# Strided attention on one core: query block 0 loaded ahead of the keys, and the first stores and reused loads in another order

## The chip, the cores and the metric

The kernel runs on one core of one Trainium2 chip. The metric is the device time of one execution in microseconds (us); the number that counts is the median of several executions. A profiled execution is recorded beside them, with its own time and with the span from its first to its last instruction.

## What is computed

Q, K and V have shape 8 x 12 x 1024 x 64 in float32, and the stride is 64. Every query attends to the same 16 positions of its head, which are rows 0, 64, 128 and so on of K and V:

```python
batch, heads, seq, dim = Q.shape              # 8, 12, 1024, 64
attend_positions = np.arange(0, seq, stride)  # 16 positions
k = K[:, :, attend_positions, :]
v = V[:, :, attend_positions, :]
scores = np.einsum('bhqd,bhkd->bhqk', q, k) / np.sqrt(dim)
weights = softmax(scores)                     # over the 16 positions
result = np.einsum('bhqk,bhkd->bhqd', weights, v)
```

All of Q is read (25.2 MB), of K and V one row of 256 bytes in 64 (0.39 MB each), and the result is as large as Q (25.2 MB).

## The kernel before

**Tiles.** The 96 heads are worked on in 24 groups of 4 heads. One group's queries are 1 MiB, 8 KB in each of 128 partitions. The tile `big` has 16 such buffers (NB = 16); group g uses buffer g modulo 16. A group's outputs are written into the buffer that its queries came in, and are stored from there. So groups 0 to 15 each have a buffer from the start, and groups 16 to 23 reuse the buffers of groups 0 to 7: their loads, the *reused loads*, can be issued only when the outputs of the old group have been stored. Keys and values are loaded into the last buffer (`k_raw`, `v_raw` are views of it), and are rearranged with the help of the one before it; queries 14 and 15 are loaded there later.

**The work of one group.** ACT and POOL each convert half of the queries to bfloat16 (`cast_a` on line 343, `cast_p` on line 348), DVE transposes them (`turn_over`, line 352), PE makes the scores (line 505), DVE transposes them and takes the maximum (lines 372 and 377), POOL subtracts it, ACT takes the exponential (line 388), DVE adds up and inverts, POOL normalises, DVE transposes the weights, PE makes the outputs (line 519) in two halves, and ACT copies each half into `big` (`evict`, line 420). A loop over n runs these steps skewed: step n holds the score work of group n, the casts of later groups (`cast_a(n + 3)`, `cast_p(n + 2)`) and the outputs of groups n - 2 and n - 3.

**The keys' way.** ACT casts the first half of the key rows and POOL the second (lines 289 and 290), DVE transposes them (line 292), DVE and ACT lay them out in `k_all` (line 299), and POOL copies a group's part into `k_cur` (line 356). Value rows are cast by POOL (line 314) and spread over the partitions by PE (line 306).

**What sets the order.** The kernel is one list of operations, written by hand in the order of the code. `op` records each with what it reads and writes; `plan` derives the semaphore waits. Each engine runs its own operations in the order of the list. All transfers are issued by SP, one after the other, on one queue; a transfer that must wait for a semaphore holds SP, and with it every later transfer. The `lane` of a transfer is the semaphore that it raises when it has landed: `q0` to `q15` for the loads, `out0` to `out7` for the stores (and for K and V, which borrow three of them).

**The transfers.** A load of queries (`load`) and a store (`store`, `send`) are issued through `_copy` (line 34), which writes the DMA instruction itself. A load reads 32 runs of 32 KB; a store takes two groups, 2 MiB. K and V go through the ordinary call `nc.sync.dma_start` (line 254) with 128 rows of 256-byte pieces. `first_loads` issues K in two halves, then queries 0, then V, then queries 1 to 13; queries 14 and 15 follow within the loop. After that the list `order` says in which order stores ("S") and reused loads ("L") are issued; `issue` is called at the end of each step and takes from the head of the list whatever is due. The store of group g waits for an ACT operation behind the eviction of the group (`at_ACT`); the reused load of group g waits for the store that frees its buffer. The very last store, of groups 22 and 23, is issued after the loop (line 560).

Of the kernel before, what the change touches and what calls it, by code (L numbers as in the profile page):

```python
# [18 lines left out]
def _ap_with(ap: bass.AP, new_ap, extra_offset: int = 0) -> bass.AP:  # L19
    return dataclasses.replace(  # L20
        ap, ap=[list(p) for p in new_ap], offset=ap.offset + extra_offset
    )
# [20 lines left out]
class Program:  # L43
# [13 lines left out]
    def op(self, engine, fn, reads=(), writes=(), after=(), lane=None, gate=None, gates=(), looped=False, last=False):  # L57
        i = len(self.ops)
        deps, own = set(after), set()
        for k in reads:  # L60
            deps.add(self.writer.get(k))
            own.add(self.writer.get(k))
        for k in writes:
            deps.update(self.readers.get(k, ()))
            deps.add(self.writer.get(k))
            own.add(self.writer.get(k))
        deps.discard(None)
        for k in reads:
            self.readers.setdefault(k, []).append(i)
        for k in writes:  # L70
            self.writer[k], self.readers[k] = i, []
        self.ops.append(dict(
            engine=engine, fn=fn, lane=lane or engine, deps=deps, own=own,
            gate=gate, gates=gates, last=last, looped=looped or engine == "PE",
        ))
        return i
# [90 lines left out]
def kernel(  # L167
# [8 lines left out]
    nc = tc.nc  # L176

    B, H, S, D = Q.shape
# [3 lines left out]
    P = 128  # L182
# [3 lines left out]
    NC = NG // 2  # L186
    SD = S * D
    NB = 16
# [10 lines left out]
    big = sb.tile([P, NB, 32 * D], FP32, name="big")  # L199
# [19 lines left out]
    k_raw = spare[:, 0 : NC * D].rearrange("p (n d) -> p n d", d=D)  # L219
    v_raw = spare[:, NC * D : 2 * NC * D].rearrange("p (n d) -> p n d", d=D)  # L220
    later_bf = later.bitcast(BF16)
    k_bf, k_r, v_bf, v_rep, v_rep2 = [
        later_bf[:, i * NC * D : (i + 1) * NC * D].rearrange("p (n d) -> p n d", d=D) for i in range(5)
    ]
# [5 lines left out]
    op = prog.op  # L230

    def load(g):
        n, b = 32, g % NB
        over = {NB - 1: ["k_raw0", "k_raw1", "v_raw"], NB - 2: ["k_bf0", "k_bf1", "k_r", "v_bf", "v_rep0", "v_rep1"]}
        op("SP", lambda: _copy(
            nc, big[:, b], _ap_with(Q, [[HG * SD // n, n], [1, HG * SD // n]], g * HG * SD),
        ), writes=[f"b{b}a", f"b{b}b"] + (over.get(g) or []), lane=f"q{b}")

    def store(g, n):
        b = g % NB  # L240
        op("SP", lambda: send(g, n), lane=f"out{b // 2}",
           reads=[f"b{i % NB}{h}" for i in range(g, g + n) for h in "ab"])

    def send(g, n):
        o = big[:, g % NB : g % NB + n]
        return _copy(
            nc,
            _ap_with(out, [[16 * D, P], [2 * SD, 2 * n], [1, 16 * D]], g * HG * SD),
            _ap_with(o, [o.ap[0], [1, 1], [1, 32 * n * D]]),
        )  # L250

    def first_loads():
        def rows(name, tile_, src, i0, n, lane):
            op("SP", lambda: nc.sync.dma_start(tile_[:, i0 : i0 + n], _ap_with(  # L254
                src, [[stride * D, P], [2 * HG * SD, n], [1, D]], 2 * HG * SD * i0,
            )), writes=[name], lane=lane)

        for m in range(2):
            rows(f"k_raw{m}", k_raw, K, NC // 2 * m, NC // 2, f"out{5 + m}")
        load(0)  # L260
        rows("v_raw", v_raw, V, 0, NC, "out7")
        for g in range(1, NB - 2):
            load(g)

    def constants():
# [20 lines left out]
        ), reads=["identity"], writes=["s_sel"])  # L286

    def key_rows():
        op("ACT", lambda: nc.scalar.copy(k_bf[:, 0:6], k_raw[:, 0:6]), reads=["k_raw0"], writes=["k_bf0"])
        op("POOL", lambda: nc.gpsimd.tensor_copy(out=k_bf[:, 6:], in_=k_raw[:, 6:]),  # L290
           reads=["k_raw1"], writes=["k_bf1"])
        op("DVE", lambda: nc.vector.transpose(
            k_r.rearrange("p n d -> p (n d)").bitcast(I32), k_bf.rearrange("p n d -> p (n d)").bitcast(I32),
        ), reads=["k_bf0", "k_bf1"], writes=["k_r"])
# [122 lines left out]
    def evict(g, h):  # L417
# [3 lines left out]
           gate=None if g == NG - 1 else "ev")  # L421

    first_loads()
    constants()
    key_rows()
    for s in range(4):
        keys(0, s, "DVE" if s < 2 else "ACT")
# [3 lines left out]
    for s in range(4):  # L431
# [8 lines left out]
    value_copy(1)  # L440
    cast_a(2)
    value_blocks(0, range(2))
    order = [("S", 0), ("S", 2), ("S", 4), ("L", 16), ("L", 17), ("S", 6), ("L", 18), ("L", 19), ("S", 8),
             ("L", 20), ("L", 21), ("S", 10), ("L", 22), ("L", 23)] + [("S", g) for g in range(12, 22, 2)]

    def issue(done, flush=False):
        while order:
            kind, g = order[0]
            need = g + (kind == "S") if kind != "L" else g - NB + 1
            if not flush and need > done:  # L450
                return
            order.pop(0)
            if kind == "L":
                load(g)
            else:
                store(g, 2)

    def on(f, g, *a):
        if 0 <= g < NG:
# [135 lines left out]
```

## Time and profile before

| | |
|---|---|
| median of 3 executions | 128.47 us (128.4 to 129.09) |
| profiled execution, its own time | 128.98 us |
| profiled execution, span | 127.2 us |
| bytes moved by DMA | 51.18 MB, mean 402 GB/s |
| busy share of the span: PE, DVE, ACT, POOL | 52%, 77%, 71%, 68% |
| mean granted TensorE clock | 0.767 |
| loads of queries, stores, loads of K, loads of V | 24, 12, 2, 1 |

In the rows of the profile, L343 is line 343 of the kernel before, `big<-in_Q_dram` a load of queries, `out_dram<-big` a store. A row of the timeline gives the start, the duration, the engine, the line, the operation, what it writes and reads, how many of them, and in brackets how long the engine had been idle before it and what ended that. A table of windows gives the busy time of each engine in stretches of the span, the granted clock (PEclk), the DMA share (mean busy share of the 16 DMA engines, by the packets that start in the stretch, so it can exceed 1) and the rate.

### The profile page before, as it was taken

What the parts mean: (1) busy time and instruction counts of PE and PEld (TensorE: products, weight loads), DVE (VectorE), ACT (ScalarE), POOL (GpSimd) and SP (SyncE); (2) the same over time, 40 slices, a digit from 0 to 9 for tenths busy, and PEclk for the clock granted to TensorE, in tenths of its full rate; (3) what the DMA queues carried; (4) which work ended last, traced back from release to release, by engine and by line L of the source; (5) the groups of instructions that cost most, each with busy time, mean ns of one, the idle gap of its engine ahead of it and who ended that gap; (6) DMA issues with size and microseconds to landing.
All of it is one profiled execution on the core that took longest, in us unless ns stands there. A gap on an engine that the chain in (4) does not pass through costs nothing.

```text
span 127.2 us, 1795 instructions
## 1 busy us (share of the span) xinstructions
PE 65.5 (52%) x580; PEld 34.5 (27%) x580; DVE 98.1 (77%) x159; ACT 90.1 (71%) x106; POOL 86.8 (68%) x132
## 2 busy tenths in 40 slices
PE   0005233489777775534578977754736777840000
PEld 0001000134444332222333544313404435420000
DVE  4473689999999999999999999959939997500000
ACT  4153759988888989999898898469469768880000
POOL 4134585999999999999999999986866968400000
PEclk9999999999999999999555555568555555586555
DMA  2999999999999999999989999989999999989990
GB/s 66 302 348 446 443 433 423 412 453 443 412 423 443 433 392 417 412 438 474 433 381 438 448 402 435 453 376 438 474 389 422 412 433 438 423 345 423 453 438 26
DMA packets 6006, 51.18 MB, mean 402 GB/s; under 512 B 3696, under 2 KB 3696, under 8 KB 3696
## 3 DMA queue, kind: packets, MB, share of 16 engines
q1 hardware_dynamic: 6000, 51.12, 96.2%
q14 instruction: 5, 0.04, 0.1%
q8 instruction: 1, 0.02, 0.0%
HBM read 25.95 MB, written 25.17 MB: 402 GB/s over the span
## 4 chain that ended last, share of the span: by engine, by line
DMA 36%; ACT 26%; PE 11%; DVE 7%; issue 7%; SPq 1%; POOL 1%
ACT big L420 20%; DMA big<-in_Q_dram 17%; DMA out_dram<-big 13%; PE o L519 9%; DMA big<-in_V_dram 6%; ACT qb L343 4%; DVE qt L352 3%; ACT ex L388 2%; PE sc L505 2%; DVE total L393 1%; DVE top L377 1%; DVE s_t L372 1%; SPq L254 1%; POOL big L314 1%; PE o L306 1%
## 5 line engine op out<-in xcount | busy, mean ns | idle before, releaser
L519 PE MATMUL o<-v_cur,w_t 64*64 64x256 bf16 x384 | 41.3, 382 | 24.6 <-ACT big L420 17.7
L420 ACT COPY big<-o 128x1024 f32<-128x1024 f32 x48 | 46.2, 1014 | 6.4 <-PE o L519 6.1
L519 PEld LDWEIGHTS o<-v_cur,w_t 64*64 64x64 bf16 x384 | 30.8, 150 | 44.4 <-ACT big L420 34.8
L343 ACT CAST qb<-big 128x1024 bf16<-128x1024 f32 x24 | 25.2, 1051 | 9.3 <-DMA big<-in_Q_dram 9.3
L402 POOL TENSOR_TENSOR w_n<-ex,rec 128x512 bf16<-128x512 f32 x24 | 25.4, 1057 | 9.4 <-DVE rec L398 9.4
L505 PE MATMUL sc<-qt,k_cur 128*32 128x512 bf16 x192 | 23.7, 587 | 11.7 <-DVE qt L352 11.7
L352 DVE STREAM_TRANSPOSE qt<-qb 128x1024 int32<-128x1024 int32 x24 | 28.9, 1205 | 0.9 <-POOL qb L348 0.9
L348 POOL CAST qb<-big 128x1024 bf16<-128x1024 f32 x24 | 25.1, 1046 | 5.5 <-DMA big<-in_Q_dram 5.4
L382 POOL TENSOR_TENSOR diff<-s_t,top 128x512 f32<-128x512 f32 x24 | 25.4, 1057 | 2.8 <-DVE top L377 2.8
L393 DVE TENSOR_REDUCE total<-ex 128x32 f32<-128x544 f32 x24 | 17.1, 712 | 4.2 <-ACT ex L388 4.2
L408 DVE STREAM_TRANSPOSE w_t<-w_n 128x512 bf16<-128x512 bf16 x24 | 18.0, 750 | 1.2 <-POOL w_n L402 1.2
L388 ACT ACTIVATE ex<-diff 128x512 f32<-128x512 f32 x24 | 15.3, 636 | 1.5 <-POOL diff L382 1.4
L372 DVE STREAM_TRANSPOSE s_t<-sc 128x512 f32<-128x512 f32 x24 | 15.9, 664 | 0.4 <-PE sc L505 0.4
L377 DVE TENSOR_REDUCE top<-s_t 128x32 f32<-128x512 f32 x24 | 15.7, 652 | 0.1
L505 PEld LDWEIGHTS sc<-qt,k_cur 128*32 128x32 bf16 x192 | 3.3, 105 | 22.3 <-DVE qt L352 21.7
L398 DVE RECIPROCAL rec<-total 128x32 f32<-128x32 f32 x24 | 7.5, 313 | 0.0
L306 PE MATMUL o<-big,perm_v 128*128 128x384 bf16 x4 | 1.5, 520 | 11.0 <-POOL big L314 11.0
L362 POOL COPY v_cur<-v_all 128x128 int32<-128x128 int32 x24 | 7.0, 293 | 0.0
L356 POOL COPY k_cur<-k_all 128x64 int32<-128x64 int32 x24 | 5.8, 241 | 1.7 <-ACT k_all L299 1.7
L306 PEld LDWEIGHTS o<-big,perm_v 128*128 128x128 bf16 x4 | 0.4, 130 | 11.3 <-POOL big L314 11.0
L335 ACT ACTIVATE v_all<-big,s_sel 128x768 bf16<-128x768 bf16 x4 | 3.5, 920 | 0.0
L330 DVE TENSOR_SCALAR v_all<-big,s_sel 128x768 bf16<-128x768 bf16 x4 | 1.6, 432 | 2.5 <-ACT qb L343 2.5
(18 smaller groups left out, 12.7 us busy)
## 6 DMA issues: line engine op xcount, KB each, us to landing
big<-in_Q_dram SPq DMA_DIRECT2D x24, 1024.0 KB, 19.0
out_dram<-big SPq DMA_DIRECT2D x12, 2048.0 KB, 16.2
big<-in_K_dram SPq DMA_DIRECT2D x2, 192.0 KB, 3.9
big<-in_V_dram SPq DMA_DIRECT2D x1, 384.0 KB, 7.3
```

Source lines behind the costliest of these rows:

```text
L343: op("ACT", lambda: nc.scalar.copy(b[:, half:], q[:, half:]), reads=[f"b{g % NB}{h}" for h in "ab"], writes=[f"qb{g % 4}1"])
L348: op("POOL", lambda: nc.gpsimd.tensor_copy(out=b[:, 0:half], in_=q[:, 0:half]), reads=[f"b{g % NB}{h}" for h in "ab"], writes=[f"qb{g % 4}0"])
L352: op("DVE", lambda: nc.vector.transpose(qt[g % 2].bitcast(I32), qb[g % 4].bitcast(I32)), reads=[f"qb{g % 4}0", f"qb{g % 4}1"], writes=[f"q ...
L372: op("DVE", lambda: nc.vector.transpose(s_t[g % 2].rearrange("p n k -> p (n k)"), sc_ps[g % 2],), reads=[f"sc{g % 2}"], writes=[f"s_t{g % ...
L382: op("POOL", lambda: nc.gpsimd.tensor_tensor(out=diff[g % 2], in0=s_t[g % 2], in1=top[g % 2].unsqueeze(2).to_broadcast([P, 32, NK]), op=AL ...
L388: op("ACT", lambda: nc.scalar.activation(out=ex[g % 2][:, :, 0:NK], in_=diff[g % 2], func=AF.Exp, bias=0.0, scale=scale,), reads=[f"diff{g ...
L393: op("DVE", lambda: nc.vector.tensor_reduce(out=total[g % 2], in_=ex[g % 2], op=ALU.add, axis=mybir.AxisListType.X,), reads=[f"ex{g % 2}"] ...
L402: op("POOL", lambda: nc.gpsimd.tensor_tensor(out=w_n[g % 2], in0=ex[g % 2][:, :, 0:NK], in1=rec[g % 2].unsqueeze(2).to_broadcast([P, 32, N ...
L408: op("DVE", lambda: nc.vector.transpose(_ap_with(w_t[g % 2], [w_t[g % 2].ap[0], [64, 8], [1, 2], [2, 32]]), w_n[g % 2].rearrange("p n k -> ...
L420: op("ACT", lambda: nc.scalar.copy(to, o), reads=[f"o{h}"], writes=[f"b{g % NB}{'ab'[h]}"], gate=None if g == NG - 1 else "ev")
L505: r = pe.matmul(sc_ps[g % 2][32 * c : 32 * c + 32], lhsT=k_cur[g % 2][:, f, b], rhs=_ap_with(qt[g % 2], [qt[g % 2].ap[0], [D, 8], [16 * D, ...
L519: r = pe.matmul(o_ps[h][half_b, t // 2, 256 * (t % 2) : 256 * (t % 2) + 256], lhsT=w_t[g % 2][half_b, 4 * h + t], rhs=v_cur[g % 2][half_b] ...
```

## The change

- The load of queries 0 is taken to the head of `first_loads`. It is issued through the ordinary call, as 128 rows of 8 KB, where it was 32 runs of 32 KB.
- K is loaded in one transfer behind it, where it was two halves ahead of it. Both casts of the key rows now wait for this one transfer.
- Queries 1 stand between K and V; before, V stood ahead of queries 1.
- Groups 0 and 1 are stored by two transfers of 1 MiB, each as soon as its group is done, and not by one of 2 MiB. Group 1's store has a semaphore of its own, `out8`.
- In the list of stores and reused loads, the first reused load stands behind the stores of groups 0 to 3. Before, it stood behind the stores of groups 0 to 5. All later reused loads move ahead by one store in the same way, and one more store comes after the last of them.

The compute operations and their order on PE, DVE, ACT and POOL are the same. Lines of the changed kernel stand one or two lower than before (cast of queries on ACT: line 344; the first load: line 258).

On SP, at the start of the program, the transfers stand as follows before (-) and now (+); big is the tile of the 16 buffers, in_Q, in_K and in_V are the inputs, and the shapes are partitions and elements:

```order
-L254 DMA big<-in_K_dram 128x6x64 x2
+L258 DMA big<-in_Q_dram 128x2048
+L254 DMA big<-in_K_dram 128x12x64
 L34 DMA big<-in_Q_dram 128x2048
 L254 DMA big<-in_V_dram 128x12x64
-L34 DMA big<-in_Q_dram 128x2048 x13
+L34 DMA big<-in_Q_dram 128x2048 x12
```

A load of queries (queries 0) now stands ahead of the keys, the keys are one transfer of 12 rows for each partition, and the load between the keys and the values is that of queries 1.

On SP, at the place where stores and reused loads begin to alternate, the kernel before has (out_dram is the result; a store of 128x4x1024 is one of two groups):

```order
L34 DMA out_dram<-big 128x4x1024 [waits at_ACT] x3
L34 DMA big<-in_Q_dram 128x2048 [waits at_out0]
L34 DMA big<-in_Q_dram 128x2048
L34 DMA out_dram<-big 128x4x1024 [waits at_ACT]
L34 DMA big<-in_Q_dram 128x2048 [waits at_out1]
```

and the changed kernel has at the same place:

```order
L34 DMA out_dram<-big 128x2x1024 [waits at_ACT] x2
L34 DMA out_dram<-big 128x4x1024 [waits at_ACT]
L34 DMA big<-in_Q_dram 128x2048 [waits at_out0]
L34 DMA big<-in_Q_dram 128x2048 [waits at_out8]
L34 DMA out_dram<-big 128x4x1024 [waits at_ACT]
L34 DMA big<-in_Q_dram 128x2048 [waits at_out1]
```

The reused load of queries 16 now has two stores of one group and one of two groups ahead of it, 4 MiB in place of 6; the load of queries 17 has a wait of its own, for the store of group 1.

```diff
--- before.py
+++ after.py
@@ -231,14 +231,14 @@
 
     def load(g):
         n, b = 32, g % NB
-        over = {NB - 1: ["k_raw0", "k_raw1", "v_raw"], NB - 2: ["k_bf0", "k_bf1", "k_r", "v_bf", "v_rep0", "v_rep1"]}
+        over = {NB - 1: ["k_raw", "v_raw"], NB - 2: ["k_bf0", "k_bf1", "k_r", "v_bf", "v_rep0", "v_rep1"]}
         op("SP", lambda: _copy(
             nc, big[:, b], _ap_with(Q, [[HG * SD // n, n], [1, HG * SD // n]], g * HG * SD),
         ), writes=[f"b{b}a", f"b{b}b"] + (over.get(g) or []), lane=f"q{b}")
 
     def store(g, n):
         b = g % NB
-        op("SP", lambda: send(g, n), lane=f"out{b // 2}",
+        op("SP", lambda: send(g, n), lane="out8" if n < 2 and b % 2 else f"out{b // 2}",
            reads=[f"b{i % NB}{h}" for i in range(g, g + n) for h in "ab"])
 
     def send(g, n):
@@ -255,11 +255,12 @@
                 src, [[stride * D, P], [2 * HG * SD, n], [1, D]], 2 * HG * SD * i0,
             )), writes=[name], lane=lane)
 
-        for m in range(2):
-            rows(f"k_raw{m}", k_raw, K, NC // 2 * m, NC // 2, f"out{5 + m}")
-        load(0)
+        op("SP", lambda: nc.sync.dma_start(big[:, 0], _ap_with(Q, [[32 * D, P], [1, 32 * D]])),
+           writes=["b0a", "b0b"], lane="q0")
+        rows("k_raw", k_raw, K, 0, NC, "out6")
+        load(1)
         rows("v_raw", v_raw, V, 0, NC, "out7")
-        for g in range(1, NB - 2):
+        for g in range(2, NB - 2):
             load(g)
 
     def constants():
@@ -286,9 +287,9 @@
         ), reads=["identity"], writes=["s_sel"])
 
     def key_rows():
-        op("ACT", lambda: nc.scalar.copy(k_bf[:, 0:6], k_raw[:, 0:6]), reads=["k_raw0"], writes=["k_bf0"])
+        op("ACT", lambda: nc.scalar.copy(k_bf[:, 0:6], k_raw[:, 0:6]), reads=["k_raw"], writes=["k_bf0"])
         op("POOL", lambda: nc.gpsimd.tensor_copy(out=k_bf[:, 6:], in_=k_raw[:, 6:]),
-           reads=["k_raw1"], writes=["k_bf1"])
+           reads=["k_raw"], writes=["k_bf1"])
         op("DVE", lambda: nc.vector.transpose(
             k_r.rearrange("p n d -> p (n d)").bitcast(I32), k_bf.rearrange("p n d -> p (n d)").bitcast(I32),
         ), reads=["k_bf0", "k_bf1"], writes=["k_r"])
@@ -440,20 +441,21 @@
     value_copy(1)
     cast_a(2)
     value_blocks(0, range(2))
-    order = [("S", 0), ("S", 2), ("S", 4), ("L", 16), ("L", 17), ("S", 6), ("L", 18), ("L", 19), ("S", 8),
-             ("L", 20), ("L", 21), ("S", 10), ("L", 22), ("L", 23)] + [("S", g) for g in range(12, 22, 2)]
+    order = [("S", 0, 1), ("S", 1, 1), ("S", 2, 2), ("L", 16, 1), ("L", 17, 1), ("S", 4, 2), ("L", 18, 1), ("L", 19, 1),
+             ("S", 6, 2), ("L", 20, 1), ("L", 21, 1), ("S", 8, 2), ("L", 22, 1), ("L", 23, 1)]
+    order += [("S", g, 2) for g in range(10, 22, 2)]
 
     def issue(done, flush=False):
         while order:
-            kind, g = order[0]
-            need = g + (kind == "S") if kind != "L" else g - NB + 1
+            kind, g, some = order[0]
+            need = g + some - 1 if kind == "S" else g - NB + 1
             if not flush and need > done:
                 return
             order.pop(0)
             if kind == "L":
                 load(g)
             else:
-                store(g, 2)
+                store(g, some)
 
     def on(f, g, *a):
         if 0 <= g < NG:
```

## The prediction

> **What bounds the kernel now.** I read the page first, then the table of windows, the chain that ended last, and the timelines of the start and the end. A difference under 0.5% (0.64 us) is about what a measurement of this kernel cannot tell from none.
>
> ```profile
> span 127.2 us, 1795 instructions
> DMA  2999999999999999999989999989999999989990
> GB/s 66 302 348 446 443 433 423 412 453 443 412 423 443 433 392 417 412 438 474 433 381 438 448 402 435 453 376 438 474 389 422 412 433 438 423 345 423 453 438 26
> q1 hardware_dynamic: 6000, 51.12, 96.2%
> ```
>
> The DMA engines are busy from the second slice to the last but one, 96.2% of the span on one queue. No compute engine is above 77%. Since the bytes are fixed, the end can only come sooner where the DMA engines are slow or idle. The windows show where:
>
> ```profile
> core 0: us, PE busy (x) PEld busy (x) DVE busy (x) ACT busy (x) POOL busy (x), PEclk, DMA share, GB/s
> 0.00:2.00 2.00, 0.00 (x0) 0.00 (x0) 0.12 (x1) 0.69 (x1) 0.56 (x6) 1.00 0.02 4
> 2.00:2.80 0.80, 0.00 (x0) 0.00 (x0) 0.80 (x1) 0.60 (x1) 0.74 (x5) 1.00 0.49 114
> 2.80:4.00 1.20, 0.00 (x0) 0.00 (x0) 1.07 (x3) 0.00 (x0) 0.16 (x1) 1.00 2.04 462
> 4.00:6.00 2.00, 0.00 (x0) 0.00 (x0) 0.51 (x2) 0.51 (x1) 0.42 (x1) 1.00 0.66 210
> 6.00:8.00 2.00, 0.00 (x0) 0.00 (x0) 1.79 (x5) 1.01 (x2) 0.27 (x2) 1.00 0.72 249
> 8.00:10.00 2.00, 0.00 (x0) 0.00 (x0) 1.04 (x4) 1.04 (x1) 1.17 (x2) 1.00 1.44 489
> 10.00:12.00 2.00, 0.99 (x4) 0.43 (x4) 1.18 (x1) 0.13 (x1) 1.01 (x2) 1.00 0.91 393
> 12.00:14.00 2.00, 1.44 (x10) 0.14 (x8) 0.36 (x2) 2.00 (x3) 1.04 (x1) 1.00 1.07 459
> 14.00:40.00 26.00, 14.74 (x120) 6.72 (x120) 25.52 (x42) 22.07 (x27) 21.78 (x30) 1.00 1.00 429
> 40.00:113.60 73.60, 48.36 (x448) 27.16 (x448) 65.70 (x107) 61.29 (x73) 59.67 (x87) 0.68 1.00 426
> 113.60:114.80 1.20, 0.00 (x0) 0.00 (x0) 0.00 (x0) 0.70 (x1) 0.00 (x0) 1.00 0.80 341
> 114.80:124.40 9.60, 0.00 (x0) 0.00 (x0) 0.00 (x0) 0.00 (x0) 0.00 (x0) 0.54 0.98 415
> 124.40:126.40 2.00, 0.00 (x0) 0.00 (x0) 0.00 (x0) 0.00 (x0) 0.00 (x0) 0.50 0.04 16
> ```
>
> From 14 to 113.6 us the DMA share is 1.00 at 426 to 429 GB/s: nothing is to be had there. Losses stand at the start (4 to 249 GB/s for most of 8 us) and in a gap at 113.6 (341 GB/s).
>
> **The start, priced.** SP's rows and the first instructions that waited for a landing:
>
> ```profile
> 0.96 1.02 SPq L254 DMA_DIRECT2D big<-in_K_dram  x2
> 2.02 0.75 SPq L34 DMA_DIRECT2D big<-in_Q_dram  x1
> 5.58 0.51 POOL L290 CAST big<-big 128x384 bf16<-128x384 f32 x1 [2.62 <-DMA big<-in_K_dram]
> 8.76 1.04 ACT L343 CAST qb<-big 128x1024 bf16<-128x1024 f32 x1 [1.00 <-DMA big<-in_Q_dram]
> 9.94 1.25 DVE L352 STREAM_TRANSPOSE qt<-qb 128x1024 int32<-128x1024 int32 x1 [0.93 <-POOL qb L348]
> 10.13 0.83 POOL L314 CAST big<-big 128x768 bf16<-128x768 f32 x1 [0.22 <-DMA big<-in_V_dram]
> 12.58 1.04 POOL L348 CAST qb<-big 128x1024 bf16<-128x1024 f32 x1 [1.45 <-DMA big<-in_Q_dram]
> ```
>
> K is complete at about 5.6, queries 0 at 8.8, V at 10.1, queries 1 at 12.6. Behind bulk, 1 MiB takes 12.6 - 10.1 = 2.45 us and the 1536 pieces of V 10.1 - 8.8 = 1.3 us, 0.4 us over the 0.92 that their 0.39 MB take at 429 GB/s. Out in front, the same number of pieces of K lasts from the first bytes at 2.0 to 5.6, which is 3.6 us, and queries 0 then need 3.2 in place of 2.45. So K at the head costs up to 3.6 - 1.3 + 3.2 - 2.45 = 3.0 us, the delay between last byte and landing included. The windows give a second figure: by 14.0 packets of 4.25 MB had started (rate times length, summed), 9.9 us at 429 GB/s; of the other 4.1, 2.0 pass before any byte and 0.8 are the price of small pieces, twice 0.4. That leaves 1.3 us of loss, a little low, since a packet is counted whole at its start.
>
> In the changed kernel queries 0 go first. They are 128 rows of 8 KB, and while they are moved (2.45 us) the small pieces of K can be got ready behind them, as those of V are now. The first bytes still come about 2.0 us into the span, 1.1 us after the first issue at 0.96, and a ramp remains: the window from 2.0 to 2.8 moved at 114 GB/s in place of 429, a loss of 0.6. K then costs 1.3, as V does. The gain lies between 1.3 - 0.6 = 0.7 and 3.0 - 0.6 = 2.4 us. Below 0.7 it falls if the first query packets stall whatever stands before them, as those of 4 to 6 us seem to (210 GB/s, 1.0 us lost): then -0.3. I take 1.4, nearer to the windows, since the landings include the delay after the last byte, which remains.
>
> **The small edits.** SP's issues come to the same number: K loses one, the first store gains one. The queue's 6000 packets are, by their counts, 32 for each load of queries, 128 for each store, 3072 pieces of K and V, and 16 for each of 39 transfers. With rows of 8 KB queries 0 go from 32 to 128 and groups 0 and 1 from 128 to 256, 224 more, or 14 for each DMA engine. V bounds their price: 96 packets of each engine took 1.3 us, at most 14 ns each, data included, so 14 cost under 0.2 us; I take nothing.
>
> **The key chain starts later.** K lands at about 2.0 + 0.6 + 2.45 + 1.3, with the landing delay about 6.9, not 5.6. The row at 5.58 moves there, with the transpose and copies behind it; ACT and POOL take the cast of queries 0 after theirs, at about 9.1 for 8.8, and the transpose at 9.94 comes some 0.4 later. V lands at 6.9 + 2.45 + 1.3, about 10.7, not 10.1. So compute starts 0.4 to 0.6 us later. While the DMA queue is full this is hidden, by work that was issued long before.
>
> **The stores and reused loads.** Whether the 1.4 us reach the end depends on what follows:
>
> ```profile
> 32.87 15.59 SPq L34 DMA_DIRECT2D out_dram<-big  x3
> 51.57 1.39 SPq L34 DMA_DIRECT2D big<-in_Q_dram  x2
> 55.00 16.32 DMA out_dram<-big
> 71.34 22.09 DMA big<-in_Q_dram
> ```
>
> The chain's last two rows are the store of groups 6 and 7 and the load of queries 22, issued when that store lands and itself landing at 93.4. Between the two landings the queue moved queries 18 and 19, a store, 20 and 21, a store, and 22: 9 MiB in 22.1 us, so 2.45 for each MiB and 4.9 for a store.
>
> The new waits stand on SP ahead of all later transfers. Queries 16 wait for store 0 alone; behind that store 1 and groups 2 and 3 are queued, 3 MiB, 7.4 us of work. Queries 17 wait for store 1, with 3 MiB behind it too (the pair and queries 16). The first bytes come 1.1 us after issue (0.96 to about 2.0), so no gap opens, and the store of groups 4 and 5 behind them on SP is not needed for another 5 us. The store of groups 2 and 3 must be there when queries 0 to 15 and both singles are through: the pair of groups 0 and 1, landed at 51.6 (its reused load was issued then), started at 46.6, so that is about 50; SP issued it between 32.9 and 48.5. Later reused loads have 9.8 us queued behind the store that they wait for.
>
> Each reused load comes 4.9 us sooner (one store fewer ahead) and 1.4 more for the start. ACT's casts of queries show who waits:
>
> ```profile
> 61.44 1.06 ACT L343 CAST qb<-big 128x1024 bf16<-128x1024 f32 x1
> 65.64 1.06 ACT L343 CAST qb<-big 128x1024 bf16<-128x1024 f32 x1
> 69.39 1.06 ACT L343 CAST qb<-big 128x1024 bf16<-128x1024 f32 x1
> 83.69 1.04 ACT L343 CAST qb<-big 128x1024 bf16<-128x1024 f32 x1 [2.89 <-DMA big<-in_Q_dram]
> 93.44 1.04 ACT L343 CAST qb<-big 128x1024 bf16<-128x1024 f32 x1 [3.08 <-DMA big<-in_Q_dram]
> 112.38 1.93 ACT L420 COPY big<-o 128x1024 f32<-128x1024 f32 x2 [0.24 <-PE o L519]
> 113.42 1.80 SPq L34 DMA_DIRECT2D out_dram<-big  x2
> ```
>
> A group takes 3.75 us (65.64 to 69.39). Without waits queries 22 would be cast at 61.4 + 7 x 3.75 = 87.7, with the later start 88.3. They will be there at 93.4 - 4.9 - 1.4 = 87.1. So these waits go. The last eviction, 20.9 us behind that cast, comes at 109 to 110.5 (queries 23 waited too) and not at 114.3.
>
> That matters in the gap. The last two stores are issued at 113.42, with the end of the evictions; the queue ran dry for the engines that were ahead. In the changed kernel they are issued at about 109 to 110; the queue, 1.4 us earlier, needs them at 113.6 - 1.4 - 1.1 = 111. The gap closes, by one to two us of slack. It is worth 1.2 x (1 - 341/426) = 0.24 us on the mean; the engines that ran latest had no gap, so I count 0.15. What moves sooner otherwise buys nothing: the bytes behind it are the same, and the end stays a stream of stores.
>
> **Sum.** 1.4 + 0.15 = 1.55 us off the profiled execution, 128.98 to 127.43. The median of before is 0.51 below that execution, so I forecast 128.47 - 1.55 = 126.9.
>
> **Rivals.**
>
> *The start does not get faster (0.17).* The stall from 4 to 6 us belongs to the first large reads and moves to 2 us. The gain is then -0.3 to 0.3, and with the gap 0.15: about 128.3. For it: 210 GB/s persists in a window where K is nearly done. Against: in that window queries 0 were issued at 2.0 behind 1536 pieces, and V, queued in the same way behind bulk, cost 1.3.
>
> *More is won (0.12).* From 124.4 to 126.4 the DMA share is 0.04: one or two engines of 16 finish late. If they lose their lag with the start, and the start gives 1.9, then 1.9 + 0.15 + 0.5 = 2.55: 125.9. Against: nothing in the change evens the engines out.
>
> *The split transfers cost something of their own: slower (0.07).* If a packet costs by the piece, or a transfer for itself, the split store and the 128 rows hold a full queue, and every later transfer with it. Idle once for the 1.1 us from issue to bytes, the kernel takes 126.9 + 1.1 = 128.0 (0.02 for about that). It decides from 2.2 us on, 1.55 of gain and 0.64: that is 157 ns for each of the 14 packets, and the time is 129.1 (0.05). Against it: V's pieces took at most 14 ns each, and the seven transfers between 71.3 and 93.4 moved 9 MiB at 427 GB/s, with no cost for each that one could see. [...]
>
> *It does not do what it says (0.03).* If a reused load still came after its cast, for instance because SP is held longer, the gap stays: 128.47 - 1.4 = 127.1, inside the forecast's range.
>
> **Numbers.** The forecast has 0.61: 126.9, with 1.4 between 0.7 and 2.0 it runs from 126.3 to 127.6. Faster by over 0.5% are the forecast, the bigger gain and the last rival, together 0.76; within 0.5% the slow start and the cheap end of the split transfers, 0.19; slower their dear end, 0.05. The range takes in the bigger gain, a little past its time, from 125.7, and the slow start down to almost no gain, 128.4.
>
> **What would show it.** Right: in the windows from 2.8 to 8 us the rate is at 350 or more throughout; queries 0 are in by about 5.5 and K by about 7; the ACT casts of queries 20 and 22 do not wait for a DMA; the last eviction ends before 112; no window near 113 is below 400 GB/s. Wrong at the start: 14.0 us reached with no more than 4.3 MB started. Wrong at the end: a gap before the last two stores, or casts that wait for reused loads. The prediction falls if the median is above 127.8 or below 125.7.

## The result and the profile after

The changed kernel takes 128.03 us, the median of 15 runs (127.78 to 128.59); the kernel before, beside it on the same chip, takes 128.75 (15 runs, 128.4 to 129.38). The ratio is 0.9948, with a 95% interval from 0.9933 to 0.9963: 0.5 to 0.9 us less. The forecast had 1.55 less. So the direction and the wide range (125.7 to 128.4) hold, and the size is a little under half. The profiled execution took 128.59 us against 128.98 before; it is the slowest of its 15, so its span tells less than the medians.

The page of the changed kernel: the span, the DMA share in 40 slices, the rate, and the one queue that moves the data.

```profile
span 126.8 us, 1795 instructions
DMA  2999999999999999999998999999899999999991
GB/s 59 341 406 432 455 413 444 434 413 465 393 444 444 403 385 447 413 460 408 413 450 357 424 481 401 393 470 424 382 429 426 424 429 429 413 434 424 424 398 57
q1 hardware_dynamic: 6224, 51.12, 96.7%
```

The 224 more packets of the forecast are there (6224 for 6000), and the queue is still the bound, busy for 96.7% of the span. The start is read from the windows:

```profile
core 0: us, PE busy (x) PEld busy (x) DVE busy (x) ACT busy (x) POOL busy (x), PEclk, DMA share, GB/s
0.00:2.00 2.00, 0.00 (x0) 0.00 (x0) 0.12 (x1) 0.68 (x1) 0.55 (x6) 1.00 0.10 12
2.00:2.80 0.80, 0.00 (x0) 0.00 (x0) 0.80 (x1) 0.60 (x1) 0.74 (x5) 1.00 0.58 92
2.80:4.00 1.20, 0.00 (x0) 0.00 (x0) 1.08 (x3) 0.00 (x0) 0.17 (x1) 1.00 0.88 341
4.00:6.00 2.00, 0.00 (x0) 0.00 (x0) 0.51 (x2) 0.00 (x0) 0.00 (x0) 1.00 0.98 346
6.00:8.00 2.00, 0.00 (x0) 0.00 (x0) 0.00 (x0) 0.00 (x0) 0.00 (x0) 1.00 1.30 445
8.00:10.00 2.00, 0.00 (x0) 0.00 (x0) 1.28 (x3) 1.24 (x3) 0.51 (x1) 1.00 0.83 288
10.00:12.00 2.00, 0.00 (x0) 0.00 (x0) 1.95 (x4) 1.34 (x2) 1.50 (x3) 1.00 1.41 498
12.00:14.00 2.00, 1.27 (x4) 0.43 (x4) 1.97 (x2) 0.41 (x1) 1.72 (x3) 1.00 0.95 410
14.00:40.00 26.00, 14.68 (x121) 6.68 (x120) 24.72 (x39) 21.72 (x27) 19.91 (x30) 1.00 1.01 435
40.00:113.60 73.60, 48.84 (x460) 26.59 (x456) 67.59 (x110) 64.12 (x75) 61.59 (x89) 0.79 1.00 422
113.60:114.80 1.20, 0.00 (x0) 0.00 (x0) 0.00 (x0) 0.00 (x0) 0.00 (x0) 1.00 1.00 423
114.80:124.40 9.60, 0.00 (x0) 0.00 (x0) 0.00 (x0) 0.00 (x0) 0.00 (x0) 0.51 0.93 396
124.40:126.40 2.00, 0.00 (x0) 0.00 (x0) 0.00 (x0) 0.00 (x0) 0.00 (x0) 0.50 0.06 25
```

By 14.0 us 4.48 MB have started (rate times length, summed) against 4.25 before: 0.23 MB, or 0.5 us at 429 GB/s. order_only below, whose start is that of before, reaches 4.35 by 14.0, so the figure differs by 0.2 us between executions of one start. By the forecast's own reckoning 3.55 us are lost up to there, not 4.1: 1.94 before any real rate, 0.87 from 2.0 to 4.0, and 0.74 from 4.0 to 14.0, where the pieces of K and V are. The gap at 113.6 is gone (423 GB/s, before 341).

The start on SP, then the first instructions that use what landed (a bracket names the wait):

```profile
0.96 0.39 SPq L258 DMA_DIRECT2D big<-in_Q_dram  x1
1.41 0.42 SPq L254 DMA_DIRECT2D big<-in_K_dram  x1
8.03 0.51 ACT L290 CAST big<-big 128x384 bf16<-128x384 f32 x1 [5.43 <-DMA big<-in_K_dram]
10.32 1.04 ACT L344 CAST qb<-big 128x1024 bf16<-128x1024 f32 x1
11.85 0.83 POOL L315 CAST big<-big 128x768 bf16<-128x768 f32 x1
```

K is complete at 8.0 us (forecast 6.9, before 5.6). V, now the fourth transfer, was issued at 3.75, and the chain that ended last gives it 8.04 us:

```profile
3.75 8.04 DMA big<-in_V_dram
```

So the first four transfers (queries 0 and 1, K and V) are through at 11.8, and V's cast starts at 11.85. Before, the last of the same four was queries 1, whose cast started at 12.58. That is 0.7 us, a second figure for the gain, and one without the windows' rounding (in order_only, with the old start, that cast starts at 12.34, so this figure too differs by 0.2 us between executions).

The rest of the changed kernel's timeline: the first eviction, the cast of queries 22, the last eviction, and SP's issue of the last two stores.

```profile
28.19 1.93 ACT L421 COPY big<-o 128x1024 f32<-128x1024 f32 x2 [0.53 <-PE o L521]
90.19 1.06 ACT L344 CAST qb<-big 128x1024 bf16<-128x1024 f32 x1
110.53 1.93 ACT L421 COPY big<-o 128x1024 f32<-128x1024 f32 x2 [0.24 <-PE o L521]
111.57 1.80 SPq L34 DMA_DIRECT2D out_dram<-big  x2
```

The first eviction was at 26.20 before, so compute is 2.0 us later, not 0.6. The cast of queries 22, at 93.44 before, no longer waits for a DMA, and the last eviction ends at 112.5, not 114.3; the forecast had 109 to 110.5.

### The profile page after: what moved, and what is told of

The parts are those of the page before. It is cut to its first block, busy times and chain, and to the rows that moved or that the text cites. A ratio compares the mean times of both kernels' runs of the same rounds, so it can differ in the third digit from the quotient of the medians.

```text
span 126.8 us, 1795 instructions
## 1 busy us (share of the span) xinstructions
PE 64.8 (51%) x580; PEld 33.7 (27%) x580; DVE 100.0 (79%) x159; ACT 90.1 (71%) x106; POOL 86.7 (68%) x132
## 3 DMA queue, kind: packets, MB, share of 16 engines
q1 hardware_dynamic: 6224, 51.12, 96.7%
## 4 chain that ended last, share of the span: by engine, by line
DVE 70%; DMA 6%; ACT 5%; PE 3%; SPq 2%; issue 1%; POOL 1%
DVE qt L353 20%; DVE w_t L409 12%; DVE total L394 11%; DVE s_t L373 11%; DVE top L378 11%; DMA big<-in_V_dram 6%; DVE rec L399 4%; ACT big L421 3%; PE o L521 3%; DVE v_all L331 2%; SPq L34 1%; ACT qb L344 1%; PE o L307 1%; POOL big L315 1%; ACT big L323 1%
## 5 line engine op out<-in xcount | busy, mean ns | idle before, releaser
L521 PEld LDWEIGHTS o<-v_cur,w_t 64*64 64x64 bf16 x384 | 30.0, 148 | 41.6 <-ACT big L421 30.0
L507 PE MATMUL sc<-qt,k_cur 128*32 128x512 bf16 x192 | 23.2, 576 | 11.9 <-DVE qt L353 11.8
L290 ACT CAST big<-big 128x384 bf16<-128x384 f32 x1 | 0.5, 512 | 5.4 <-DMA big<-in_K_dram 5.4
L291 POOL CAST big<-big 128x384 bf16<-128x384 f32 x1 | 0.5, 509 | 5.1 <-DMA big<-in_K_dram 5.1
```

What stands on the lines that cost most here:

```text
L507: r = pe.matmul(sc_ps[g % 2][32 * c : 32 * c + 32], lhsT=k_cur[g % 2][:, f, b], rhs=_ap_with(qt[g % 2], [qt[g % 2].ap[0], [D, 8], [16 * D, ...
L521: r = pe.matmul(o_ps[h][half_b, t // 2, 256 * (t % 2) : 256 * (t % 2) + 256], lhsT=w_t[g % 2][half_b, 4 * h + t], rhs=v_cur[g % 2][half_b] ...
```

## The experiments

Two theories at first. STREAM: the end is set by the bytes in the queue, so the gain is what the start loses less, and it is small because the first query reads are slow themselves. LATE COMPUTE: the start gives the 1.4 us, and compute that begins 2 us later takes some of it back at the end. A third, GAP, gives the closed gap and the order a share of the gain. Later ones (PLACE, FIRST READS, ORDER COSTS) are about what makes the start cheaper, and what becomes of a start that is cheaper still. Each ratio stands against runs of the kernel before on the same chip, with its 95% interval.

**The two halves apart.** start_only keeps the new loads and takes the old order back:

```diff
-    order = [("S", 0, 1), ("S", 1, 1), ("S", 2, 2), ("L", 16, 1), ("L", 17, 1), ("S", 4, 2), ("L", 18, 1), ("L", 19, 1),
+    order = [("S", 0, 2), ("S", 2, 2), ("S", 4, 2), ("L", 16, 1), ("L", 17, 1), ("S", 6, 2), ("L", 18, 1), ("L", 19, 1),
...
```

> The changed start (queries 0 first, keys in one transfer, queries 1 ahead of the values) with the old order of stores and reused loads. Three theories of the measured gain of 0.7 us. STREAM: the end is set by the DMA stream, and the gain is what the stream loses less at its start, about 0.65 us; this kernel then has nearly all of it, 0.5 to 0.8 us faster than before, with a gap still ahead of the last two stores. LATE COMPUTE: the start saves more, but compute begins 2 us later and takes it back at the end; with the old order the casts wait for the reused loads as well, and this kernel is at most 0.3 us faster. GAP: the start's gain is lost again on the way, and what is left comes from the closed gap before the last stores; this kernel is within 0.2 us of before.

128.05 us against 128.86, ratio 0.994 (0.9923 to 0.9958). Its last two stores are issued a microsecond after the changed kernel's:

```profile
112.55 1.80 SPq L34 DMA_DIRECT2D out_dram<-big  x2
```

The whole gain is in the start. order_only is the other half: the old `first_loads` (K in halves, queries 0 in 32 KB runs) under the new order.

> The old start (keys in two halves, then queries 0) with the new order of stores and reused loads. STREAM: 0 to 0.2 us faster than before; the gap before the last two stores closes, but the engines that end last had none. LATE COMPUTE: compute starts as early as before and the reused loads come 4.9 us earlier, so the last eviction comes at about 110; 0.2 us faster at most, as the stream has its old start. GAP: 0.4 to 0.7 us faster than before, the whole of the measured gain.

128.85 against 128.86, ratio 1.000 (0.998 to 1.0021). Yet its profile shows what the order was to do: the last stores are issued 4 us earlier than before (109.46, not 113.42), and the gap is closed.

```profile
109.46 1.80 SPq L34 DMA_DIRECT2D out_dram<-big  x2
```

```profile
113.60:114.80 1.20, 0.00 (x0) 0.00 (x0) 0.00 (x0) 0.00 (x0) 0.00 (x0) 0.50 1.03 437
114.80:124.40 9.60, 0.00 (x0) 0.00 (x0) 0.00 (x0) 0.00 (x0) 0.00 (x0) 0.50 0.96 410
124.40:126.40 2.00, 0.00 (x0) 0.00 (x0) 0.00 (x0) 0.00 (x0) 0.00 (x0) 0.50 0.10 41
```

From 124.4 the DMA share is 0.10. The packets' records say what that is: at 125.2 three of the 16 engines still work and the last ends at 125.7, where before one still worked and ended at 126.0. The engines that ran ahead have no pause now (before, at 114.5, five of the 16 worked; here the window from 113.6 moves at 437 GB/s for 341) and finish earlier (six work at 124.4, before all 16); the last ones end about as before. GAP falls. The order also holds the price of the split store, one transfer more in a full queue, and it is nothing that can be measured.

**Does the late compute cost anything?** late_compute lengthens the key chain on ACT by five copies, of 544 numbers each, into a new tile that is allocated ahead of the buffers:

```diff
+    pad = sb.tile([P, 544], FP32, name="pad")
...
+    for _ in range(5):
+        op("ACT", lambda: nc.scalar.copy(pad, ex[0].rearrange("p n k -> p (n k)")), reads=["ex0"], writes=["pad"])
```

> The changed kernel with five copies of 544 elements more on ACT behind the cast of the key rows, so that ACT's copies of the keys and its first cast of queries come about 2.3 us later and all groups after them. STREAM: the last two stores are then issued about 2.3 us later than at 111.6, near the point at which the queue runs dry; the end moves by less than 0.5 us. LATE COMPUTE: the end moves by the delay, 1.5 to 2.3 us.

129.84 against 128.72, ratio 1.0075 (1.0049 to 1.0101), which looked like proof of LATE COMPUTE. But the new tile also moves the address of every buffer. Two kernels part these: shift_only has the unused tile and no copies; late_compute_same_place has the copies, with the tile behind all others.

> The changed kernel with the unused tile of 2176 bytes ahead of the buffers and nothing else. If the address of the buffers makes reads slower: 24 loads with two packets each on every engine, 22 ns more each, 1.06 us slower than the changed kernel. If the slower reads of the first late run were a matter of that execution: no difference.

> The late compute again, with the additional tile behind all others, so that every buffer keeps its address; five copies of 544 elements on ACT delay all groups by about 2.3 us. In the first such run reads were 2% slower from the start (1.24 us and not 1.218 for 32 KB), as the tile had moved the buffers. STREAM: less than 0.5 us slower than the changed kernel. LATE COMPUTE: 1.5 us slower or more.

shift_only alone: 129.89 against 128.67, ratio 1.0082 (1.0059 to 1.0106). late_compute_same_place: 128.18, ratio 0.9957 (0.994 to 0.9974), by the ratios 0.1 us from the changed kernel, with intervals that overlap. Its evictions begin 2 us later still, and its queue runs nearly dry before the last stores:

```profile
30.13 1.93 ACT L422 COPY big<-o 128x1024 f32<-128x1024 f32 x2 [0.52 <-PE o L524]
113.63 1.80 SPq L34 DMA_DIRECT2D out_dram<-big  x2
```

```profile
113.60:114.80 1.20, 0.00 (x0) 0.00 (x0) 0.00 (x0) 0.92 (x2) 0.00 (x0) 0.50 0.14 55
114.80:124.40 9.60, 0.00 (x0) 0.00 (x0) 0.00 (x0) 0.00 (x0) 0.00 (x0) 0.50 1.03 437
124.40:126.40 2.00, 0.00 (x0) 0.00 (x0) 0.00 (x0) 0.00 (x0) 0.00 (x0) 0.50 0.00 0
```

At 55 GB/s the window lost 1.2 x (1 - 0.14) = 1.0 us of the mean engine's work, where the gap of before lost 0.24, and the kernel is not measurably slower: in this execution no packet of data starts after 124.4, and the last engine ends at 125.0, where in the profiled execution of the changed kernel engines end between 123.3 and 125.6 (0.06 of the share after 124.4, 25 GB/s). So LATE COMPUTE falls, by the medians, and with it the price that the forecast put on the gap. The profiles suggest, and no run shows it alone, that the pause is paid back by a more even end. They are not a clean pair, though: the one execution took 127.99 us, the fastest of its nine, and the other 128.59, the slowest of its 15.

**What makes the start cheaper.** first_by_copy puts queries 0 first, but reads them as before, 32 runs of 32 KB:

```diff
-        op("SP", lambda: nc.sync.dma_start(big[:, 0], _ap_with(Q, [[32 * D, P], [1, 32 * D]])),
-           writes=["b0a", "b0b"], lane="q0")
+        load(0)
```

> The changed kernel, but queries 0 are loaded in 32 runs of 32 KB, like all the others, and not in 128 rows of 8 KB. If the size of the first packets matters (the first reads of 8 KB took about 1 us each at the start, later ones 0.31), the first bytes of larger packets come no later, but each engine's first packet is a quarter of its load or more: 0.1 to 0.4 us slower than the changed kernel. If only the place of the load matters: within 0.1 us of the changed kernel. GAP and LATE COMPUTE say nothing on it, except that a later landing of queries 0 makes no difference by GAP.

128.42 against 128.86, ratio 0.9966 (0.995 to 0.9981): by the ratios 0.2 us slower than the changed kernel, with intervals that overlap. Its windows show a slower stretch from 4 to 6 us (346 GB/s in the changed kernel), though by 14.0 us it has started 4.48 MB, as much as the changed kernel:

```profile
2.00:2.80 0.80, 0.00 (x0) 0.00 (x0) 0.80 (x1) 0.60 (x1) 0.74 (x5) 1.00 0.64 174
2.80:4.00 1.20, 0.00 (x0) 0.00 (x0) 1.07 (x3) 0.00 (x0) 0.16 (x1) 1.00 0.80 328
4.00:6.00 2.00, 0.00 (x0) 0.00 (x0) 0.51 (x2) 0.00 (x0) 0.00 (x0) 1.00 0.82 304
```

rows_of_8k_only is the kernel before with one edit: queries 0, still behind K, in 128 rows of 8 KB.

> The kernel before with one edit: queries 0, still behind the two halves of the keys, are loaded as 128 rows of 8 KB by the ordinary call. PLACE: within 0.2 us of before. FIRST READS: 0.3 to 0.8 us faster than before, since the large reads of queries 0 were what stalled from 4 to 6 us.

128.64 against 128.79, ratio 0.999 (0.9972 to 1.0008): alone, nothing measurable. keys_first is the changed kernel with K and queries 0 changed about, and keys_first_old_order the same under the old order:

```diff
+        rows("k_raw", k_raw, K, 0, NC, "out6")
         op("SP", lambda: nc.sync.dma_start(big[:, 0], _ap_with(Q, [[32 * D, P], [1, 32 * D]])),
            writes=["b0a", "b0b"], lane="q0")
-        rows("k_raw", k_raw, K, 0, NC, "out6")
```

> The changed kernel with its first two transfers swapped: keys in one transfer, then queries 0 in 128 rows of 8 KB. PLACE (small pieces in front cost more than behind bulk, as the forecast had it): 0.5 us or more slower than the changed kernel. FIRST READS (the first reads of queries take about 1 us longer wherever they stand, and pieces of K in front can run meanwhile): as fast as the changed kernel or up to 0.4 us faster, at 127.6 to 128.1, and K lands 2 us sooner.

> The same start with the old order of stores and reused loads. PLACE: 0.5 us slower than the run with the changed start and the old order (128.05). FIRST READS: 127.6 to 128.1. In either case within 0.2 us of the run beside it.

128.37 against 128.79, ratio 0.997 (0.9946 to 0.9993), and 128.25, ratio 0.9961 (0.9944 to 0.9979). So with the keys in front most of the gain may be left: beside the changed kernel and start_only the ratios put the place of K at about 0.3 us, (0.997 - 0.9948) x 128.75, with intervals that overlap. That lies between what PLACE and FIRST READS expected, and the forecast had priced K at the head at up to 3.0. The windows of keys_first show why it is so little:

```profile
2.00:2.80 0.80, 0.00 (x0) 0.00 (x0) 0.80 (x1) 0.60 (x1) 0.74 (x5) 1.00 0.25 63
2.80:4.00 1.20, 0.00 (x0) 0.00 (x0) 1.07 (x3) 0.00 (x0) 0.17 (x1) 1.00 0.94 213
4.00:6.00 2.00, 0.00 (x0) 0.00 (x0) 0.51 (x2) 0.41 (x1) 0.38 (x1) 1.00 1.04 326
6.00:8.00 2.00, 0.00 (x0) 0.00 (x0) 1.70 (x5) 1.12 (x3) 0.22 (x2) 1.00 1.19 508
```

The pieces of K are slower from 2.0 to 4.0 (63 and 213 GB/s for 92 and 341), but then the queries catch up, 508 for 445, and by 14.0 us the sum is 4.48 MB again. The casts of K, of queries 0 and of V in keys_first say the same, and beside them stands the cast of queries 0 in order_only, with the old start:

```profile
5.59 0.51 ACT L290 CAST big<-big 128x384 bf16<-128x384 f32 x1 [2.99 <-DMA big<-in_K_dram]
8.03 1.04 ACT L344 CAST qb<-big 128x1024 bf16<-128x1024 f32 x1 [0.18 <-DMA big<-in_Q_dram]
11.84 0.83 POOL L315 CAST big<-big 128x768 bf16<-128x768 f32 x1 [2.58 <-DMA big<-in_V_dram]
```

```profile
8.52 1.04 ACT L343 CAST qb<-big 128x1024 bf16<-128x1024 f32 x1 [0.65 <-DMA big<-in_Q_dram]
```

K and queries 0 together are in at 8.03 here, as in the changed kernel, where K was the later one, and V at 11.84 or 11.85. With the old start they are in at 8.76 (before) and 8.52 (order_only). K itself lands as with the old start, 5.59 and 5.58; queries 0 behind it take 2.4 us in place of 3.2 and 2.8. From there on nothing differs: V and queries 1 take 3.8 us in either order (8.76 to 12.58, 8.03 to 11.85). So the gain of the start lies in this one step. Executions differ by 0.3 us here: K and queries 0 are in at 8.33 in keys_first_old_order, at 7.78 in start_only and 7.69 in first_by_copy. With K in front that is 0.5 us sooner than with the old start on the mean, and with queries 0 in front another 0.3, as the ratios have it.

keys_first_old_order differs from rows_of_8k_only (same chip, 128.25 against 128.64) in two edits only: K in one transfer, and queries 1 ahead of V. No run takes either of the two alone into the kernel before. Two more of this kind. keys_in_halves sends K behind queries 0 in its two old halves; first_in_halves sends queries 0 as two transfers of 128 rows of 4 KB.

> The changed kernel with the keys in two transfers of half the size behind queries 0, each cast waiting for its own half. STREAM: within 0.15 us of the changed kernel, the pieces are the same. LATE COMPUTE: the first half lands some 0.6 us sooner, but the transpose waits for both casts, so compute gains 0.2 us at most, and so does the end.

> The changed kernel with queries 0 loaded as two transfers of 128 rows of 4 KB. First packets of 32 KB were 0.4 us slower at the end than first packets of 8 KB. If the first packet of each engine is what the start loses (1 us for 8 KB where 0.31 is normal), smaller ones lose less: 0.1 to 0.3 us faster than the changed kernel. If the first reads take about 1 us whatever their size: 0 to 0.1 us slower, for the added transfer.

128.15, ratio 0.9945 (0.9927 to 0.9963), and 128.16, ratio 0.9959 (0.9936 to 0.9982). Neither edit costs or gains anything that can be told from the changed kernel.

**A start without pieces.** wide_rows reads K and V as 128 rows of 3 KB, other rows of the same size; so its output is not the reference's.

```diff
-                src, [[stride * D, P], [2 * HG * SD, n], [1, D]], 2 * HG * SD * i0,
+                src, [[n * D, P], [D, n], [1, D]], 0,
```

> The changed kernel, but of K and V the first 128 rows of 3 KB are read in one piece each, where 1536 pieces of 256 bytes were read: the same number of bytes, in 128 packets and not 1536 (other rows than the reference's are attended to). It measures what the small pieces still cost behind bulk. STREAM, with the price of the forecast (0.4 us for K and 0.4 for V): 0.8 us faster than the changed kernel, at 127.2. With the trace of the changed kernel, where 0.65 was lost while K ran and 0.43 while V ran: 1.1 us faster. LATE COMPUTE: the keys land up to 0.6 us sooner, and no more than that is won.

128.38 against 128.72, ratio 0.9964 (0.9941 to 0.9987): no better. Yet its start is, and by 14.0 us 4.98 MB are under way, 1.15 us ahead of the changed kernel. One of its windows at the start, and one further on, where it reads queries 15:

```profile
4.00:6.00 2.00, 0.00 (x0) 0.00 (x0) 0.51 (x2) 0.00 (x0) 0.00 (x0) 1.00 1.04 426
...
42.00:45.00 3.00, 2.49 (x23) 1.14 (x18) 3.00 (x5) 2.64 (x4) 3.00 (x5) 1.00 0.85 243
```

In the changed kernel the last window moved at 385 GB/s; (385 - 243) x 3.0 / 429 is 1.0 us, nearly the whole lead. In the packets' records 16 reads of 32 KB take 1.9 to 2.2 us each there, where 1.22 is usual. ORDER COSTS blamed the new order; wide_rows_old_order has the old one.

> The kernel with wide rows of K and V (K and V as 128 rows of 3 KB, other rows than the reference's), but with the old order of stores and reused loads. With wide rows the stream was 1.2 us further at 40 us than in the changed kernel, yet the end came no sooner. ORDER COSTS (the reads that follow stores in the new order run slower, and eat what the start gives): here the gain stays, 1.5 to 2.0 us faster than before, near 127.0. FLOOR (something holds the end at about 128 whatever the start gives): 128.0 to 128.4, as with the new order.

128.12 against 128.67, ratio 0.9949 (0.993 to 0.9968), and the same slow window:

```profile
42.00:45.00 3.00, 2.46 (x22) 1.13 (x18) 3.00 (x5) 2.63 (x4) 3.00 (x5) 1.00 0.91 279
```

So it is not the new order. What slows these reads stays open.

**The pieces beside the stream.** kv_on_act issues K and V on ACT's own queue (`nc.scalar.dma_start`), with the queries on SP's; kv_on_act_old_order is the same under the old order.

> The changed kernel, but K and V are issued by ACT at the start of the program, on ACT's own queue, while SP issues only queries. Both queues are then served side by side from 2 us on. STREAM: the first query packets, which took about 1 us each at the start of the changed kernel, have pieces of K beside them, and the pieces have query packets beside them; part of the 0.9 us lost before 3 us and of the 1.1 us lost on pieces is won: 0.3 to 1.0 us faster than the changed kernel. If an engine serves one packet at a time whatever the queue: within 0.2 us of it. LATE COMPUTE: keys and values land earlier, near 5 to 7 us, so compute starts up to 2 us earlier and the end comes earlier by a good part of that, whatever the stream does.

> K and V on ACT's queue as in the run beside it, with the old order of stores and reused loads. STREAM: the order was worth nothing with the old start; so this is within 0.2 us of the run beside it. If the new order loses on its reads what it gains at the gap, as the traces so far show it, the same. LATE COMPUTE: slower than the run beside it by 0.3 us or more, since the casts wait for the reused loads again.

157.32, ratio 1.2197 (1.2162 to 1.2233), and 157.27, ratio 1.2204 (1.2171 to 1.2238). ACT's rows and the page's rates (slices of 3.9 us) tell it:

```profile
1.34 3.00 ACTq L254 DMA_DIRECT2D big<-in_K_dram  x1
4.38 28.74 ACTq L254 DMA_DIRECT2D big<-in_V_dram  x1
39.62 0.51 ACT L290 CAST big<-big 128x384 bf16<-128x384 f32 x1 [5.17 <-DMA big<-in_K_dram]
```

```profile
GB/s 135 462 426 409 443 410 435 418 409 340 98 0 0 0 0 405 337 337 0 337 337 371 371 438 384 430 451 396 466 396 417 430 428 426 426 421 97 405 405 270
```

K is complete only at 39.6 us, after the 14 loads of SP's queue, and ACT stands in its issue of V for 28.7 us; compute begins 31.6 us late, and the queue is empty for four slices. For each DMA engine the loads are 26 packets of 32 KB and 8 of 8 KB, K is 96 pieces. In the packets' records each engine starts 30 pieces from 10 to 35 us, beside 20 reads of 32 KB: three pieces for two large reads, so that two thirds of K are left when the loads are nearly through. What sets that proportion, no run shows. By the ratios K and V on ACT's queue cost 29 us against the changed kernel, (1.2197 - 0.9948) x 128.75.

## Why the prediction came out so

**Direction and place: right.** The kernel is faster, the queue is the bound, the start is where it loses, and start_only shows the whole gain there.

**The size of the start, and what it is made of: wrong.** The step that failed is "I take 1.4, nearer to the windows, since the landings include the delay after the last byte, which remains". Measured are 0.5 us by the windows, 0.7 by the first four transfers, 0.7 by the medians and 0.8 by start_only: the lower end, 0.7, was the answer. Behind that step stands the price of K at the head, 1.3 by the windows and up to 3.0 by the landings. Keys_first leaves K there and still has K and queries 0 in at 8.03: the place of K is worth about 0.3 us, by the ratios and by the rows, and is not told apart from none. The rest of the gain, 0.4 to 0.5 us, came with the other edits of the start.

- *The ramp, 0.6 forecast, 0.87 measured (2.0 to 4.0 us).* The forecast took the one window from 2.0 to 2.8 for all of the ramp. With queries 0 in front that window is no better (92 GB/s, before 114), and the next is still short (341). In the packets' records of the changed kernel only six reads of queries start before 2.5 us, on 16 engines, and six of the first sixteen reads of 8 KB take 0.85 to 1.4 us each; the usual one takes 0.31. Queries 0 land at 6.8 (the trace's record of landings), not by 5.5 as the forecast had it, and K 1.2 behind them, as forecast.
- *The pieces, 0.8 forecast, 0.74 measured.* Right: behind bulk K costs no more than V, 1.2 us behind queries 0 for V's 1.3 behind queries 1 (landings at 6.8 and 8.0, 10.5 and 11.8). That a piece takes at most 14 ns was misread, since the pieces of V start at 7.2, before queries 0 have landed. In the packets' records the median piece takes 18 ns, of K and of V, in front (before) and behind bulk (changed kernel).

The upper end, 2.4, counted costs that do not go away. It read 3.6 us between first bytes and K's landing as the price of the pieces, but 96 pieces take an engine 1.7 us in either place; the rest is the slow start, which the changed kernel pays with queries 0 in front, and the delay until the landing is recorded, 0.3 us in either place (last piece of K through at 5.2 and landing at 5.5 before, 7.7 and 8.0 in the changed kernel). The other part of that upper end, queries 0 taking 3.2 in place of 2.45, is of the size of the gain; but keys_first wins most of it with K still in front. In the packets' records of before, nine of the first sixteen reads of queries 0, of 32 KB, take 2.0 to 2.5 us each (1.22 is usual). So the rival *the start does not get faster* was right in part: some of the stall does move to 2 us, but not all of it, since 0.7 us are won and it had 0.3 at most.

**The gap, 0.15 forecast: nothing.** It closed as foreseen, and order_only puts it at 0 within about 0.26 us. Late_compute_same_place agrees, with a larger gap (55 GB/s, 1.0 us of the mean engine's work) and no loss that can be measured (ratio 0.9957 for 0.9948). The forecast half saw it ("the engines that ran latest had no gap") and counted 0.15 all the same.

**The order: as forecast in kind, later in time.** The casts of queries wait for no DMA (before 9.3 us in all), and the reused loads come in time. The last eviction, at 112.5 for 109 to 110.5, misses mainly because compute began 2.0 us later, not 0.4 to 0.6, after K had landed at 8.0, not 6.9. In order_only, with the old start, the last stores do go out at 109.5, as the forecast's figure had it.

**The later compute, nothing forecast: right.** Late_compute_same_place delays it 2 us more, for 0.1 us by the ratios, which is not told apart from none.

**The split transfers, nothing forecast: right.** In order_only one more store in the full queue costs nothing that can be measured (ratio 1.000), and in rows_of_8k_only the 128 rows cost nothing that can be measured (0.999).

**By its own bounds** the prediction falls: 128.03 is above the 127.8 that it set, and above the 127.6 to which the forecast itself ran. It lies within the range only because that was drawn down to 128.4 to take in the slow start. The windows it named came close (341 and 346 GB/s where it asked for 350), and 4.48 MB had started by 14.0, more than the 4.3 that would have refuted the start.

**Open.** How the 0.7 us divide between the edits of the start: the place of queries 0, their 8 KB rows, K in one transfer, and queries 1 ahead of V. By the ratios, with the other edits kept, the place is worth 0.3 us, the rows of 8 KB 0.2 and K in one transfer nothing; none of these is told apart from none. Queries 1 ahead of V, which all the faster starts share, were never put back, and only the rows say that their place costs nothing. Why some reads run slow in mid-run, so that wide_rows loses its lead. Which DMA engines end last, and why. No kernel tried here is measurably faster than the changed one; start_only, with the old order, equals it.

## What to carry to other kernels

When a transfer is moved out of the head of a queue, price the head itself first: here what the first transfer cost for being first stayed, and fell to the one that took its place (by the windows from 2.0 to 4.0 us, 1.3 us lost with K in front in keys_first, 0.87 with queries 0 in the changed kernel, and 4.48 MB started by 14.0 in both). Where two bounds differ because one of them holds that cost, the smaller is the safer forecast. A gap in which only part of the DMA engines idle was worth nothing here (11 of 16 at most, closed in order_only for a ratio of 1.000); count it only when the engines that end last are shown in it. And when a change has several edits at one place, take each of them alone out of it and alone into the kernel before: here more than half of the gain, by the medians, was left when the edit that named the change was taken out.

## What the runs showed of the hardware

An unused tile of 2176 bytes in each partition ahead of the buffers makes the kernel 1.7 us slower than the changed one by the ratios (1.0082 and 0.9948), and 1.7 slower than late_compute_same_place on the same chip (129.89 against 128.18), whose added tile stands behind the others. The lines of shift_only:

```profile
q1 hardware_dynamic: 6224, 51.12, 97.0%
```

```profile
14.00:40.00 26.00, 12.27 (x114) 4.91 (x114) 23.56 (x38) 21.73 (x26) 19.61 (x27) 0.96 1.01 422
```

The same packets occupy the engines for 97.0% of 128.2 us, which is 124.4, not 96.7% of 126.8, which is 122.6, and the loads run at 422 GB/s in place of 435. In the packets' records the usual read of 32 KB takes 1.24 us in place of 1.22. Which addresses are slow was not tried. So an edit that adds a tile must be timed with the buffers left where they were; late_compute alone would have been misread. The second surprise is kv_on_act above: on a second queue each DMA engine started 30 small pieces beside 20 large reads from 10 to 35 us, and K was complete at 39.6 us, for 8.0.
